# Second expert choice over 54 key-score sums, and places turned into rows and columns by steps, in a two-layer encoder with product-key experts

## The chip, the core and the metric

The kernel runs on one core of a Trainium2 chip, in one launch. The metric is the device time of one execution in microseconds (us), lower is better. TensorE does the matrix products, VectorE (DVE) and ScalarE (ACT) the elementwise work, GpSimd (POOL) issues the indirect DMAs here, and SyncE (SP) the plain DMAs. Each engine works through its own queue in order.

## The reference, cut to what matters

256 tokens of width 1024 pass through two layers. Each has a token mixer (two attention branches, left out here) and a product-key expert layer, which the change touches:

```python
q = (xc @ w_query).reshape(T, 8, 2, 128)              # 8 heads, two half queries
s = einsum('thpk,pnk->thpn', q, sub_keys)             # 128 key scores for each half
sv, si = lax.top_k(s, 16)
cand = sv[:, :, 0, :, None] + sv[:, :, 1, None, :]    # 16 x 16 sums
cidx = si[:, :, 0, :, None] * 128 + si[:, :, 1, None, :]
top_s, sel = lax.top_k(cand, 16)                      # the second choice, of 256
eidx = take_along_axis(cidx, sel)
g = softmax(top_s)
act = gelu(einsum('td,thkd->thk', x, expert_down[eidx]))
out = einsum('thk,thkd->td', g * act, expert_up[eidx])
```

Since both lists of 16 are sorted, the sum at place (a, b) can be among the 16 largest only if (a+1)(b+1) is at most 16.

## The kernel before

**Products.** All weights stream in units of 128 x 1024 values (512 KB). Each is split into a rounded part `wh` (ScalarE, L194) and a rest `wl` (VectorE, L197), up to four units ahead, and TensorE multiplies three combinations of parts. In the expert layer the down weights of all 16384 experts are multiplied (128 units, two to a block, 64 blocks, L1326, products at L1338 to L1340, 24 to a unit). Of the up weights, the rows that some token uses are gathered in an order found on the chip and multiplied at L1372.

**Choosing experts**, while query and down products run: `score_lane` (L929) makes the key scores. `topk_lane` (L943) has eight steps per layer (four head pairs by two chunks of 128 tokens). In each, `top16` (L909: two rounds of the eight largest, their places, and a replacement of the first eight) sorts four rows of 128 scores in two pairs, then two rows of 256 sums (made at L958). `index_lane` (L966) follows when the eighth step is done, chunk by chunk: it parts each chosen place (0 to 255) into row and column by a shift and a mask, compares these with 0 to 15 (`i16`, L989), multiplies by the key numbers (L992), and adds up 16 values by halving sums (L995: 1024, 512, 256 and 128 values). TensorE then turns the result round (L1005) and it goes to `ijT` and `gT` (the last at L1015). When both chunks are through, `done["idx"]` is set; before block 32 the down products require it (`main_need("idx")`, L1329).

**From `idx` on.** `gate_lane` (L1091) starts the gate groups (`gate_group`, L1026): one-hot matrices on VectorE and ScalarE and products of them on TensorE, 44 groups for list 0 (80 of the 128 rows of experts), then 32 for list 1. `rank_lane` (L1107) counts which experts are used and ranks them when the last group of a list is done (products at L1134, L1139 and L1143, between them a ScalarE copy at L1136). `send_lane` (L1166) then has GpSimd send the 80 (or 40) rows of gate times activation to their ranked places (L1183). `read_back` (L1201) reads a list's rows back when all its sends have landed, `split_rows` (L1247) splits them (L1259, L1261), the number read with a row gathers its up weights (L1243), and `Stream._prep` (L186) splits those at L194 and L197.

**Order.** A planner in the kernel's Python (`Lanes`, L67) writes out one order for all engines. It has a clock each for TensorE ("p"), VectorE ("v") and ScalarE ("s"). A lane is a generator whose `yield ("v", cost)` says what the instructions behind it cost. A step is put in when its engine's clock and the lane's due time are at most `far` ahead of "p" (4.0 us, 6.0 for the splits), and its lane is due again 0.15 after it. `main` adds the products' cost to "p" (0.7 for a quarter of a down unit) and lets the lanes go on. `vcost(n)` is 0.1 + 0.00105 n; a split costs 1.14 of "v". The costs set the order alone, the chip its own times.

Of the kernel before, what the change touches and what calls it, by code (L numbers as in the profile page):

```python
# [12 lines left out]
F16 = mybir.dt.float16  # L13
U32 = mybir.dt.uint32
AF = mybir.ActivationFunctionType
OP = mybir.AluOpType
# [14 lines left out]
NU_W = 34 + 8 + 8 + 16  # L31


C_ID, C_IOTA, C_I16, C_COS, C_SIN, C_MA, C_MB, C_END = 0, 128, 256, 272, 400, 528, 592, 1104


GSCALE, LOW = 2.0 ** 15, 2.0 ** -11
NQ = 4
AHEAD = 4

# [18 lines left out]
def vcost(n):  # L59
    return 0.1 + n * 0.00105  # L60
# [159 lines left out]
def encoder_kernel(ctx, tc, x_in, wts, downs, ups, gains, gate_bias, qk_norm, rpb, sink, skeys, consts, sums, out,  # L220
                   depth=DEPTH):
    nc = tc.nc
    ctx.enter_context(tc.manual_schedule())
    cpool = ctx.enter_context(tc.tile_pool(name="cpool", bufs=1))
# [74 lines left out]
    x = cpool.tile([128, 2, D], F32, name="x")  # L299
    cst = cpool.tile([128, C_COS], F32, name="cst")  # L300
    TT = cpool.tile([128, 2, 2, 8, 128], F32R, name="TT")
    TTf = TT.rearrange("p c l k t -> p (c l k t)")
    iota2 = cpool.tile([128, 128, 2], F16, name="iota2")
    i16 = cpool.tile([128, 8, 2], F16, name="i16")
    tiny = cpool.tile([128, 2], F32, name="tiny")
    rank = cpool.tile([128, 128], U32, name="rank")
    miss = cpool.tile([128, 4], F16, name="miss")
# [160 lines left out]
    for l in range(depth):  # L468
# [5 lines left out]
        if l == 0:  # L474
            g1n = z[:, 0, 0:4, :].rearrange("p a b -> p (a b)")
            nc.sync.dma_start(g1n, bcast_row(gains, 0, D))
            nc.sync.dma_start(cst, consts[:, 0:C_COS])
            st.load(0)
            nc.sync.dma_start(x[:, 1, :], x_in[128:256, :])
            st.load(3)  # L480

            nc.vector.memset(iota2, 0.0)
            z2 = iota2.rearrange("p a b -> p (a b)")
            warm = take("s")
            for n in range(40):
# [12 lines left out]
            nc.vector.tensor_copy(iota2, cst[:, C_IOTA:C_IOTA + 128][:, :, None].to_broadcast([128, 128, 2]))  # L498
            nc.vector.tensor_copy(i16.rearrange("p a s -> p (a s)"), cst[:, C_I16:C_I16 + 16])
            acc_first = first_half(u, "T1")  # L500

        ctab = ap.tile([128, C_END - C_COS], F32, name="ctab")
# [373 lines left out]
        def area(off, n, u32=False):  # L876
            return (afu if u32 else afl)[:, A0 + off:A0 + off + n]
# [45 lines left out]
        sv = [area(M + ch * 768, 256).rearrange("p (q k) -> p q k", k=16) for ch in range(2)]  # L923
# [3 lines left out]
        M2 = M + 1536  # L927
# [15 lines left out]
        def topk_lane():  # L943
            for n in range(8):
                cg, ch = n // 2, n % 2
                yield from lane_need([("s", cg, ch)])
                sc = area(4096 + n * 512, 512).rearrange("p (q n) -> p q n", n=128)
                s2 = area(8192 + (n % 2) * 512, 512).rearrange("p (q n) -> p q n", n=128)
                cd = area(9216 + (n % 2) * 512, 512).rearrange("p (h a b) -> p h a b", h=2, b=16)
                c2 = area(10240 + (n % 2) * 512, 512).rearrange("p (h ab) -> p h ab", h=2)  # L950
                for k in range(0, 4, 2):
                    yield ("v", 2.0)
                    top16([(sv[ch][:, 4 * cg + j, :], si[ch][:, 4 * cg + j, :], sc[:, j, :], s2[:, j, :])
                           for j in (k, k + 1)])
                yield ("v", 0.7)
                for hh in range(2):
                    h = 2 * cg + hh
                    nc.vector.tensor_tensor(cd[:, hh], sv[ch][:, 2 * h, :, None].to_broadcast([128, 16, 16]),  # L958
                                            sv[ch][:, 2 * h + 1, None, :].to_broadcast([128, 16, 16]), op=OP.add)
                yield ("v", 3.4)  # L960
                top16([(ts[ch][:, 2 * cg + hh, :], sel[ch][:, 2 * cg + hh, :],
                        cd[:, hh].rearrange("p a b -> p (a b)"), c2[:, hh]) for hh in range(2)])
                if n == 7:
                    done["top"] = 0.0

        def index_lane():  # L966
            yield from lane_need(["top"])
            for ch in range(2):
                w = lambda k: area(M2 + k * 128, 128).rearrange("p (h k) -> p h k", k=16)
                wu = lambda k: area(M2 + k * 128, 128, True).rearrange("p (h k) -> p h k", k=16)  # L970
                sif = area(M2 + 8 * 128, 128).bitcast(F16).rearrange("p (h q k) -> p h q k", q=2, k=16)
                wh = lambda k: area(M2 + k * 128, 128).bitcast(F16).rearrange("p (n s) -> p n s", s=2)
                yield ("v", 0.6)
                nc.vector.tensor_tensor(w(0), ts[ch], ts[ch][:, :, 0:1].to_broadcast([128, 8, 16]), op=OP.subtract)
                nc.vector.tensor_copy(sif, si[ch].rearrange("p (h q) k -> p h q k", q=2))
                te = yield ("s", 0.3)
                nc.scalar.activation(w(0), w(0), AF.Exp)
                yield ("v", 0.8)
                nc.vector.tensor_scalar(wu(1), sel[ch], 4, None, op0=OP.logical_shift_right)
                nc.vector.tensor_scalar(wu(7), sel[ch], 15, None, op0=OP.bitwise_and)  # L980
                for k in range(2):
                    nc.vector.tensor_copy(wh(2 + k), area(M2 + (1, 7)[k] * 128, 128, True)[:, :, None].to_broadcast(
                        [128, 128, 2]))
                for q in range(2):

                    eq = area(11264, 1024).bitcast(F16).rearrange("p (n a s) -> p n a s", a=8, s=2)
                    e4 = area(11264, 1024).bitcast(F16).rearrange("p (h k a) -> p h k a", h=8, a=16)
                    yield ("v", vcost(1024) + 0.3)
                    nc.vector.tensor_tensor(eq, wh(2 + q)[:, :, None, :].to_broadcast([128, 128, 8, 2]),  # L989
                                            i16[:, None, :, :].to_broadcast([128, 128, 8, 2]), op=OP.is_equal)  # L990
                    yield ("v", vcost(1024))
                    nc.vector.tensor_mul(e4, e4, sif[:, :, q, None, :].to_broadcast([128, 8, 16, 16]))  # L992
                    for m in (8, 4, 2, 1):
                        yield ("v", vcost((64 if m > 1 else 128) * m))
                        nc.vector.tensor_add(w(4 + q)[:, :, :, None] if m == 1 else e4[:, :, :, 0:m], e4[:, :, :, 0:m],  # L995
                                             e4[:, :, :, m:2 * m])
                sm = area(M2 + 7 * 128, 8)
                yield ("v", 0.8)
                nc.vector.tensor_reduce(sm, w(0), axis=AX.X, op=OP.add)
                nc.vector.reciprocal(sm, sm)  # L1000
                nc.vector.tensor_mul(w(6), w(0), sm[:, :, None].to_broadcast([128, 8, 16]))
                b, = yield from lane_take("t")
                yield ("p", 0.65)
                for k in range(3):
                    nc.tensor.transpose(b[:, k * 128:(k + 1) * 128], area(M2 + (4 + k) * 128, 128), ident)  # L1005
                cs = slice(ch * 128, (ch + 1) * 128)
                yield ("s", 0.6)
                nc.scalar.activation(ijT[:, :, cs], b[:, 0:256].rearrange("p (a t) -> p a t", a=2), AF.Copy)
# [317 lines left out]
        for b in range(64):  # L1326
# [4 lines left out]
            for ii in range(2):  # L1331
                h, lo = st.get(u)
# [167 lines left out]
def const_table():  # L1500
    c = np.zeros((128, C_END), np.float32)
    c[:, C_ID:C_ID + 128] = np.eye(128, dtype=np.float32)
    c[:, C_IOTA:C_IOTA + 128] = np.arange(128, dtype=np.float32)[None]
    c[:, C_I16:C_I16 + 16] = np.arange(16, dtype=np.float32)[None]
    half = DH // 2
    inv = np.float32(10000.0) ** (-np.arange(half, dtype=np.float32) / np.float32(half))
    ang = np.arange(T, dtype=np.float32)[:, None] * inv[None, :].astype(np.float32)
# [36 lines left out]
```

## Time and profile before

| what | before |
|---|---|
| median of 3 runs | 1828.98 us (1825.52 to 1829.77) |
| the profiled execution | 1823.0 us, its span 1821.2 us |
| TensorE busy | 1774.6 us (97%) |
| VectorE busy | 1476.7 us (81%) |
| ScalarE busy | 1084.8 us (60%) |
| GpSimd busy | 503.6 us (28%) |
| DMA | 377.4 MB, 207 GB/s in the mean |

The span is the profiled execution from its first to its last instruction, and the time has 1.8 us more around it. Issuing instructions and waits are not counted as busy. Matmuls overlap in their pipeline and their ends are modelled.

### The profile page before, as it was taken

To read this page: it belongs to the slowest core of one execution; us is meant where nothing else is said; L and a number is where in the kernel's file an instruction comes from. 1 tells how busy PE (TensorE), PEld (TensorE's weight loads), DVE (VectorE), ACT (ScalarE), POOL (GpSimd) and SP (SyncE) were. 2 spreads that over 40 slices of the span, in tenths; PEclk is the share of its full clock that TensorE was granted. 3 is DMA by queue.
4 is the path that set the end of the run, shared out by engine and by line. 5 is a ranking of instruction groups with operands and counts; after the bars stand their busy time and mean duration, and the time that the engine had idled before them with its cause. 6 is when DMAs were issued, how large, how long until landed. Compare 5 with 4: busy or idle time off the path is not lost. (4 is left out here: it accounts for less than half of the span.)

```text
span 1821.2 us, 37929 instructions
## 1 busy us (share of the span) xinstructions
PE 1774.6 (97%) x14646; PEld 1619.0 (89%) x14646; DVE 1476.7 (81%) x3196; ACT 1084.8 (60%) x1784; POOL 503.6 (28%) x448
## 2 busy tenths in 40 slices
PE   8999999999999989999999999999999999799998
PEld 7889899999999978878778988999999999788786
DVE  6986799998888967766689768999888889677665
ACT  5675554676557646665646654546665577466554
POOL 0000000000007777775200000000000177677661
PEclk9999999999999989999999999999999999899999
DMA  7535455544547869989564354556444588699893
GB/s 258 162 114 167 149 155 184 196 157 149 160 143 239 250 216 349 322 303 342 190 213 143 106 164 162 162 182 201 149 153 153 158 240 250 244 327 321 302 324 129
DMA packets 130518, 377.40 MB, mean 207 GB/s; under 512 B 17552, under 2 KB 43792, under 8 KB 130320
## 3 DMA queue, kind: packets, MB, share of 16 engines
q1 hardware_dynamic: 90288, 239.26, 42.7%
q0 software_dynamic: 40032, 135.54, 20.5%
q8 instruction: 119, 1.95, 0.4%
q14 instruction: 79, 0.65, 0.1%
HBM read 341.98 MB, written 32.75 MB: 206 GB/s over the span
## 5 line engine op out<-in xcount | busy, mean ns | idle before, releaser
L197 DVE TENSOR_TENSOR wl<-raw,wh 128x1024 fp32r<-128x1024 f32 x476 | 577.9, 1222 | 144.1 <-ACT wh L194 135.7
L194 ACT ACTIVATE wh<-raw 128x1024 fp32r<-128x1024 f32 x476 | 503.1, 1058 | 252.7 <-PE bank L1372 60.9
L1338 PE MATMUL bank<-TT,wh 128*128 128x256 f32 x2048 | 586.2, 286 | 0.0
L1340 PE MATMUL bank<-TT,wl 128*128 128x256 f32 x2048 | 572.9, 280 | 2.2 <-DVE wl L197 2.2
L1339 PE MATMUL bank<-TT,wh 128*128 128x256 f32 x2048 | 571.8, 279 | 0.0
L1340 PEld LDWEIGHTS bank<-TT,wl 128*128 128x128 f32 x2048 | 385.6, 188 | 3.9 <-DVE wl L197 3.9
L1339 PEld LDWEIGHTS bank<-TT,wh 128*128 128x128 f32 x2048 | 385.8, 188 | 0.0
L1338 PEld LDWEIGHTS bank<-TT,wh 128*128 128x128 f32 x2048 | 385.2, 188 | 0.3
L1372 PE MATMUL bank<-wh,TT 128*128 128x512 f32 x1296 | 358.4, 396 | 5.1 <-DVE TT L1261 2.1
L1183 POOL DMA_INDIRECT rows<-act,rank x240 | 280.6, 1169 | 92.5 <-issue 62.8
L1372 PEld LDWEIGHTS bank<-wh,TT 128*128 128x128 f32 x1296 | 242.3, 188 | 69.5 <-DVE TT L1261 6.1
L881 POOL IOTA act<- 128x128 uint32 (+2 forms) x6 | 2.0, 332 | 1080.0 <-PE bank L361 410.2
L197 DVE TENSOR_TENSOR wl<-act,wh 128x1024 fp32r<-128x1024 f32 x126 | 154.4, 1226 | 81.3 <-ACT wh L194 81.2
L1372 PE MATMUL bank<-wl,TT 128*128 128x512 f32 x648 | 204.8, 395 | 0.8 <-issue 0.8
L194 ACT ACTIVATE wh<-act 128x1024 fp32r<-128x1024 f32 x126 | 133.4, 1060 | 103.0 <-PE bank L1372 90.0
L1243 POOL DMA_INDIRECT act<-in_ups_dram,act x118 | 132.3, 1121 | 74.2 <-issue 28.1
L1372 PEld LDWEIGHTS bank<-wl,TT 128*128 128x128 f32 x648 | 121.7, 188 | 29.4
L441 PE MATMUL bank<-TT,wh 128*128 128x256 f32 x448 | 128.6, 287 | 2.0 <-ACT raw_ka L570 1.0
L443 PE MATMUL bank<-TT,wh 128*128 128x256 f32 x448 | 125.1, 279 | 0.0
L444 PE MATMUL bank<-TT,wl 128*128 128x256 f32 x448 | 125.0, 279 | 0.0
L1282 ACT ACTIVATE act<-bank 128x256 f32<-128x256 f32 (+12 forms) x214 | 65.5, 351 | 80.3 <-PE bank L1340 78.0
L1043 ACT ACTIVATE oh<-oh 128x1024 f16<-128x1024 f16 (+2 forms) x108 | 102.0, 958 | 14.5 <-DVE oh L1040 13.4
(262 smaller groups left out, 2835.7 us busy)
## 6 DMA issues: line engine op xcount, KB each, us to landing
raw<-in_downs_dram SPq DMA_DIRECT2D x256, 512.0 KB, 3.7
raw<-in_wts_dram SPq DMA_DIRECT2D x132, 512.0 KB, 4.3
act<-rows SPq DMA_DIRECT2D x100, 129.0 KB, 5.0
act<-rows SPq DMA_DIRECT2D x98, 64.5 KB, 5.1
act<-in_ups_dram SPq DMA_DIRECT2D x8, 512.0 KB, 7.3
raw<-in_ups_dram SPq DMA_DIRECT2D x8, 512.0 KB, 6.5
rows<-act,rank POOLq DMA_INDIRECT x240, 5.0
act<-in_ups_dram,act POOLq DMA_INDIRECT x118, 6.8
```

The costliest lines, as they stand in the source:

```text
L194: self.nc.scalar.activation(h, r, AF.Copy)
L197: self.splits.append(self.nc.vector.tensor_sub(lo, r, h.bitcast(F32)).ins.name)
L441: nc.tensor.matmul(o, wh, rh, start=first and i == 0 and pc == 0, stop=False, skip_group_check=True)
L443: nc.tensor.matmul(o, wh, rl, start=False, stop=False, skip_group_check=True)
L444: nc.tensor.matmul(o, wl, rh, start=False, stop=last and i == len(kcs) - 1 and pc == 1, skip_group_check=True)
L1043: nc.scalar.activation(el, ej, AF.Copy, scale=LOW)
L1183: snd = nc.gpsimd.indirect_dma_start(byrank[r], bass.IndirectOffsetOnAxis(ap=rank[:, i:i + 1], axis=0), afl[:, i * ROW:(i + 1) * ROW], None)
L1243: nc.gpsimd.indirect_dma_start(w, None, ups_rows, bass.IndirectOffsetOnAxis(ap=num, axis=0), element_offset=l * 16384 * D)
L1338: nc.tensor.matmul(o, lh, TT[:, :, 0, kc, :], start=kc == 0, stop=False)
L1339: nc.tensor.matmul(o, lh, TT[:, :, 1, kc, :], start=False, stop=False)
L1340: nc.tensor.matmul(o, ll, TT[:, :, 0, kc, :], start=False, stop=kc == 7)
L1372: nc.tensor.matmul(oacc[ch][hf], a, r[:, hf * 512:(hf + 1) * 512], start=first[hf] and a is lh and r is h, stop=last and a is ll)
```

## The change

The second choice is taken from 54 sums instead of 256. `STEPS` lists rectangles (first row, rows, columns): one row with 16 columns, one with 8, two with 5, four with 3 and eight with 1. These hold every place with (a+1)(b+1) up to 16. Five additions, each for two heads, write them one behind the other, and `top16` sorts rows of 54.

A place is now a number from 0 to 53, and row and column no longer come from a shift and a mask. For each place all 16 row starts (`c16[:, 1]`) are compared with it (`is_ge`). The outcome times the differences of successive row keys (`dif`), added up, gives the row's key number; times the differences of successive row starts (`c16[:, 2]`), added up, it gives the start of its row. The place less that start is the column, which is compared with 0 to 15 as before. There are three times four halving sums per chunk instead of twice four, and five passes over 2048 f16 values instead of four. A second buffer of 1024 words holds the outcome of the comparison. The costs in the `yield`s change with it. The constant table has 32 more columns.

```diff
+STEPS = [(0, 1, 16), (1, 1, 8), (2, 2, 5), (4, 4, 3), (8, 8, 1)]
+CANDS = sum(n * m for _, n, m in STEPS)
...
-                cd = area(9216 + (n % 2) * 512, 512).rearrange("p (h a b) -> p h a b", h=2, b=16)
-                c2 = area(10240 + (n % 2) * 512, 512).rearrange("p (h ab) -> p h ab", h=2)
+                cd = area(9216 + (n % 2) * 512, 2 * CANDS).rearrange("p (h c) -> p h c", h=2)
+                c2 = area(10240 + (n % 2) * 512, 2 * CANDS).rearrange("p (h c) -> p h c", h=2)
...
-                yield ("v", 0.7)
-                for hh in range(2):
-                    h = 2 * cg + hh
-                    nc.vector.tensor_tensor(cd[:, hh], sv[ch][:, 2 * h, :, None].to_broadcast([128, 16, 16]),
-                                            sv[ch][:, 2 * h + 1, None, :].to_broadcast([128, 16, 16]), op=OP.add)
-                yield ("v", 3.4)
...
+                yield ("v", 0.9)
+                s4 = sv[ch][:, 4 * cg:4 * cg + 4, :].rearrange("p (h q) k -> p h q k", q=2)
+                c0 = 0
+                for a0, na, nb in STEPS:
+                    shape = [128, 2, na, nb]
+                    nc.vector.tensor_tensor(cd[:, :, c0:c0 + na * nb].rearrange("p h (a b) -> p h a b", a=na),
+                                            s4[:, :, 0, a0:a0 + na, None].to_broadcast(shape),
+                                            s4[:, :, 1, None, 0:nb].to_broadcast(shape), op=OP.add)
+                    c0 += na * nb
+                yield ("v", 2.2)
+                top16([(ts[ch][:, 2 * cg + hh, :], sel[ch][:, 2 * cg + hh, :], cd[:, hh], c2[:, hh])
+                       for hh in range(2)])
...
-                yield ("v", 0.6)
+                yield ("v", 1.2)
                 nc.vector.tensor_tensor(w(0), ts[ch], ts[ch][:, :, 0:1].to_broadcast([128, 8, 16]), op=OP.subtract)
                 nc.vector.tensor_copy(sif, si[ch].rearrange("p (h q) k -> p h q k", q=2))
+
+                nc.vector.tensor_copy(dif[:, :, 0:1], sif[:, :, 0, 0:1])
+                nc.vector.tensor_sub(dif[:, :, 1:16], sif[:, :, 0, 1:16], sif[:, :, 0, 0:15])
                 te = yield ("s", 0.3)
                 nc.scalar.activation(w(0), w(0), AF.Exp)
-                yield ("v", 0.8)
-                nc.vector.tensor_scalar(wu(1), sel[ch], 4, None, op0=OP.logical_shift_right)
-                nc.vector.tensor_scalar(wu(7), sel[ch], 15, None, op0=OP.bitwise_and)
...
+                yield ("v", 0.3)
+                nc.vector.tensor_copy(pl(1), sel[ch].rearrange("p h k -> p (h k)")[:, :, None].to_broadcast([128, 128, 2]))
...
+                yield ("v", vcost(1024))
+                nc.vector.tensor_tensor(g8, pl(1)[:, :, None, :].to_broadcast([128, 128, 8, 2]),
+                                        c16[:, 1, None, :, :].to_broadcast([128, 128, 8, 2]), op=OP.is_ge)
+                yield ("v", vcost(1024))
+                nc.vector.tensor_mul(e4, g4, dif[:, :, None, :].to_broadcast([128, 8, 16, 16]))
+                yield from total(w(4)[:, :, :, None])
+
+                yield ("v", vcost(1024))
+                nc.vector.tensor_mul(e8, g8, c16[:, 2, None, :, :].to_broadcast([128, 128, 8, 2]))
+                yield from total(pl(2).rearrange("p (h k) s -> p h k s", h=8)[:, :, :, 0:1])
+                yield ("v", 0.6)
+                nc.vector.tensor_sub(pl(3)[:, :, 0:1], pl(1)[:, :, 0:1], pl(2)[:, :, 0:1])
+                nc.vector.tensor_copy(pl(3)[:, :, 1:2], pl(3)[:, :, 0:1])
+                yield ("v", vcost(1024))
+                nc.vector.tensor_tensor(e8, pl(3)[:, :, None, :].to_broadcast([128, 128, 8, 2]),
+                                        c16[:, 0, None, :, :].to_broadcast([128, 128, 8, 2]), op=OP.is_equal)
+                yield ("v", vcost(1024))
+                nc.vector.tensor_mul(e4, e4, sif[:, :, 1, None, :].to_broadcast([128, 8, 16, 16]))
+                yield from total(w(5)[:, :, :, None])
```

`total` is the four halving sums, each behind its own `yield ("v", vcost(...))`, with the last one into the place given.

## Rows read from the trace of the kernel before

**Rows 1.** The page, busy us, share of the span and instructions of each engine.
```profile
PE 1774.6 (97%) x14646; PEld 1619.0 (89%) x14646; DVE 1476.7 (81%) x3196; ACT 1084.8 (60%) x1784; POOL 503.6 (28%) x448
```
**Rows 2.** Waits of weight loads, whole span: total us, times, longest.
```profile
PEld L1143 <- ACT scr L1136: 19.1, 2, 10.0
...
PEld bank L1340 <- DVE wl L197: 3.9, 8, 0.6
```
**Rows 3.** The same view, from 205 to 350 us.
```profile
PEld bank L1340 <- DVE wl L197: 2.0, 4, 0.6
```
**Rows 4.** Stretches: busy us (instructions) of PE, PEld, DVE, ACT, POOL, clock, DMA.
```profile
211.00:321.00 110.00, 109.21 (x926) 108.60 (x925) 109.91 (x435) 53.38 (x75) 0.00 (x0) 1.00 0.52 164
321.00:366.50 45.50, 45.13 (x384) 44.92 (x384) 43.43 (x69) 28.19 (x43) 0.37 (x1) 1.00 0.61 195
...
660.00:680.00 20.00, 11.03 (x99) 10.13 (x98) 7.68 (x23) 5.76 (x11) 11.88 (x13) 0.74 0.74 243
```
**Rows 5.** Timeline, ScalarE, 658 to 690 us: start, us, instruction, idle before.
```profile
666.95 0.61 ACT L1259 ACTIVATE wh<-act 128x256 fp32r<-128x256 f32 x2 [5.34 <-DMA act<-rows]
673.14 1.06 ACT L194 ACTIVATE wh<-raw 128x1024 fp32r<-128x1024 f32 x1 [5.58 <-DMA raw<-in_ups_dram,act]
674.10 0.57 ACT L1136 ACTIVATE scr<-bank 40x512 f16<-40x512 f32 x1
```
**Rows 6.** GpSimd: first and last send of layer 0, and their group.
```profile
544.20 2.15 POOL L1183 DMA_INDIRECT rows<-act,rank  x1 [9.70 <-DVE miss L1155]
...
662.17 0.96 POOL L1183 DMA_INDIRECT rows<-act,rank  x1 [0.30 <-issue]
...
L1183 POOL DMA_INDIRECT rows<-act,rank x80 | 94.9, 1186 | 33.8 <-issue 18.6 <-DVE miss L1155 9.7 <-DVE oh L1049 4.0
```
**Rows 7.** Timeline, TensorE, 674 to 679 us.
```profile
674.73 0.51 PE L1143 MATMUL bank<-scr 40*128 40x40 f16 x10 [8.97 <-ACT scr L1136]
...
677.69 0.41 PE L1340 MATMUL bank<-TT,wl 128*128 128x256 f32 x1
...
677.99 0.89 PE L1372 MATMUL bank<-wh 128*128 128x512 f32 x2
```
**Rows 8.** Timeline, VectorE, index lane of layer 0.
```profile
320.93 2.33 DVE L197 TENSOR_TENSOR wl<-raw,wh 128x1024 fp32r<-128x1024 f32 x2
...
352.19 2.18 DVE L995 TENSOR_TENSOR act<-act 128x1024 f16<-128x1024 f16 x4
...
365.78 0.23 DVE L1015 TENSOR_SCALAR gT<-act 128x128 f16<-128x128 f32 x1
```
**Rows 9.** Timeline, VectorE, one step of the top-k lane.
```profile
237.21 0.48 DVE L912 MAX8 act<-act 128x8 f32<-128x128 f32 x2
...
239.56 1.21 DVE L197 TENSOR_TENSOR wl<-raw,wh 128x1024 fp32r<-128x1024 f32 x1
...
244.16 0.75 DVE L958 TENSOR_TENSOR act<-act 128x256 f32<-128x256 f32 x2
244.82 0.74 DVE L912 MAX8 act<-act 128x8 f32<-128x256 f32 x2
...
248.51 2.34 DVE L197 TENSOR_TENSOR wl<-raw,wh 128x1024 fp32r<-128x1024 f32 x2
250.76 0.48 DVE L912 MAX8 act<-act 128x8 f32<-128x128 f32 x2
```
**Rows 10.** Timeline, VectorE, two small steps of the rank lane.
```profile
535.65 0.20 DVE L1128 TENSOR_TENSOR scr<-scr 128x80 f16<-128x80 f16 x1
535.77 0.19 DVE L1129 TENSOR_TENSOR scr<-scr 128x80 f16<-128x80 f16 x1
```
**Rows 11.** Groups by form: count, busy us, mean ns, idle before.
```profile
L197 DVE TENSOR_TENSOR wl<-raw,wh 128x1024 fp32r<-128x1024 f32 x476 | 577.9, 1222 | 144.1 <-ACT wh L194 135.7 <-DVEq L1387 5.0
...
L958 DVE TENSOR_TENSOR act<-act 128x256 f32<-128x256 f32 x32 | 12.1, 422 | 0.0
...
L989 DVE TENSOR_TENSOR act<-act,i 128x2048 f16<-128x2048 f16 x8 | 9.8, 1220 | 0.1
```

More of the change, by code (lines that the diff above doesn't have):

```diff
@@ L31 @@
 NU_W = 34 + 8 + 8 + 16
-C_ID, C_IOTA, C_I16, C_COS, C_SIN, C_MA, C_MB, C_END = 0, 128, 256, 272, 400, 528, 592, 1104
+C_ID, C_IOTA, C_I16, C_COS, C_SIN, C_MA, C_MB, C_END = 0, 128, 256, 304, 432, 560, 624, 1136
 GSCALE, LOW = 2.0 ** 15, 2.0 ** -11
+STEPS = [(0, 1, 16), (1, 1, 8), (2, 2, 5), (4, 4, 3), (8, 8, 1)]
+CANDS = sum(n * m for _, n, m in STEPS)
 NQ = 4
@@ L303, in encoder_kernel @@
     iota2 = cpool.tile([128, 128, 2], F16, name="iota2")
-    i16 = cpool.tile([128, 8, 2], F16, name="i16")
+    c16 = cpool.tile([128, 3, 8, 2], F16, name="c16")
     tiny = cpool.tile([128, 2], F32, name="tiny")
@@ L498, in encoder_kernel @@
             nc.vector.tensor_copy(iota2, cst[:, C_IOTA:C_IOTA + 128][:, :, None].to_broadcast([128, 128, 2]))
-            nc.vector.tensor_copy(i16.rearrange("p a s -> p (a s)"), cst[:, C_I16:C_I16 + 16])
+            nc.vector.tensor_copy(c16.rearrange("p n a s -> p (n a s)"), cst[:, C_I16:C_I16 + 48])
             acc_first = first_half(u, "T1")
@@ L954, in topk_lane @@
                            for j in (k, k + 1)])
-                yield ("v", 0.7)
-                for hh in range(2):
-                    h = 2 * cg + hh
-                    nc.vector.tensor_tensor(cd[:, hh], sv[ch][:, 2 * h, :, None].to_broadcast([128, 16, 16]),
-                                            sv[ch][:, 2 * h + 1, None, :].to_broadcast([128, 16, 16]), op=OP.add)
-                yield ("v", 3.4)
-                top16([(ts[ch][:, 2 * cg + hh, :], sel[ch][:, 2 * cg + hh, :],
-                        cd[:, hh].rearrange("p a b -> p (a b)"), c2[:, hh]) for hh in range(2)])
+                yield ("v", 0.9)
[10 more added lines that the diff above has]
+                       for hh in range(2)])
                 if n == 7:
@@ L971, in index_lane @@
                 sif = area(M2 + 8 * 128, 128).bitcast(F16).rearrange("p (h q k) -> p h q k", q=2, k=16)
-                wh = lambda k: area(M2 + k * 128, 128).bitcast(F16).rearrange("p (n s) -> p n s", s=2)
-                yield ("v", 0.6)
+                dif = area(M2 + 9 * 128, 64).bitcast(F16).rearrange("p (h k) -> p h k", h=8)
+                pl = lambda k: area(M2 + k * 128, 128).bitcast(F16).rearrange("p (n s) -> p n s", s=2)
+                yield ("v", 1.2)
                 nc.vector.tensor_tensor(w(0), ts[ch], ts[ch][:, :, 0:1].to_broadcast([128, 8, 16]), op=OP.subtract)
@@ L981, in index_lane @@
[L981 to L992, printed above, removed]
+                yield ("v", 0.3)
@@ L993, in index_lane, with total @@
+                nc.vector.tensor_copy(pl(1), sel[ch].rearrange("p h k -> p (h k)")[:, :, None].to_broadcast([128, 128, 2]))
+                ge, eq = [area(11264 + k * 1024, 1024).bitcast(F16) for k in range(2)]
+                g8, e8 = [x.rearrange("p (n a s) -> p n a s", a=8, s=2) for x in (ge, eq)]
+                g4, e4 = [x.rearrange("p (h k a) -> p h k a", h=8, a=16) for x in (ge, eq)]
+                def total(dst):
                     for m in (8, 4, 2, 1):
                         yield ("v", vcost((64 if m > 1 else 128) * m))
-                        nc.vector.tensor_add(w(4 + q)[:, :, :, None] if m == 1 else e4[:, :, :, 0:m], e4[:, :, :, 0:m],
-                                             e4[:, :, :, m:2 * m])
+                        nc.vector.tensor_add(dst if m == 1 else e4[:, :, :, 0:m], e4[:, :, :, 0:m], e4[:, :, :, m:2 * m])
@@ L1503, in const_table @@
     c[:, C_IOTA:C_IOTA + 128] = np.arange(128, dtype=np.float32)[None]
-    c[:, C_I16:C_I16 + 16] = np.arange(16, dtype=np.float32)[None]
+    first = np.concatenate([[0], np.cumsum(sum(([m] * n for _, n, m in STEPS), []))[:-1]])
+    c[:, C_I16:C_I16 + 48] = np.concatenate([np.arange(16), first, np.diff(first, prepend=0)])[None]
     half = DH // 2
```

## Prediction

> **What bounds the kernel now.** The page first: TensorE is busy in 97% of the span, VectorE in 81% [rows 1]. So VectorE time as such is worth nothing; what counts is where TensorE stands still, 46.6 us in all (1821.2 less 1774.6). I therefore read the waits of TensorE and its weight loads next. One of them is large: in each layer the products at L1143 wait some 9.5 us for ScalarE's copy at L1136, 19.1 us in two waits [rows 2]. A smaller one bears on the changed code: a down product (L1340) waits for VectorE's `wl` (L197) eight times, 3.9 us [rows 2], and four of these, 2.0 us, lie in layer 0 between 205 and 350 us [rows 3]; the other four stand in the same stretch of layer 1.
>
> The stretches say why. While the key scores are sorted (211 to 321 us) VectorE is busy 109.9 of 110 us, so the splits that TensorE needs come late; in the index stretch behind it 43.4 of 45.5 us [rows 4].
>
> The large wait is 300 us later and has another cause. In the slice from 660 to 680 us TensorE is busy 11.0 of 20 us and its granted clock falls to 0.74 of full speed [rows 4]. ScalarE's queue has, in this order, the splits of the first rows read back (L1259, idle 5.3 us for a DMA), the split of the first gathered up block (L194, idle 5.6 us for the gather) and then L1136 [rows 5]. The gather waits for rows read back, and those for the last of 80 row sends. The sends run on GpSimd one behind the other from 544.2 to 663.1 us: 94.9 us of work and about 0.3 us between two, which is 119 us for 80 [rows 6]. They start when the first list's ranks are known, at the end of the gate groups, which start at `done["idx"]`. So **the time at which the index lane ends, in TensorE's own program, sets when the stall at L1143 ends** (674.7 us) [rows 7], as long as gates and sends keep their lengths. Nothing waits at `main_need("idx")`: the index lane ends at 366 us [rows 8], and block 32 is some 179 us of products behind the first (32 times two units of 2.8 us), which begins only after the 12 query units that run beside the first sorts.
>
> **The change, part by part. Sorting on the engine.** One step of the top-k lane (eight a layer) runs from 237.2 to 250.8 us [rows 9]. A pair of 128-wide sorts takes 2.35 us (237.21 to 239.56), the two 256-wide sums 0.66, the 256-wide sorts 3.69 (244.82 to 248.51). Ten sort instructions lose (3.69-2.35)/128 = 10.5 ns per column together, so 54 columns cost 3.69 - 202 x 0.0105 = 1.6 us if the line holds; at worst they cost as much as the 128-wide ones, 2.35. The five small sums (16 to 32 values each) show nowhere; the nearest rows are 80-wide f16 steps of 0.2 us started 0.12 us apart [rows 10], against 0.33 us for a 256-wide sum, so 5 x 0.13 = 0.65, at most 5 x 0.42 = 2.1 [rows 11]. I take the line and 0.65, since the operands are small and independent: a step falls by 3.69 + 0.66 - 1.6 - 0.65 = 2.1 us (bounds -0.1 and 2.2), 16 steps by 33.6 us.
>
> [...]
>
> **Index lane on the engine.** Added per chunk: one cast and two shifts less (some 0.4 together, at the 0.12 to 0.2 of small steps [rows 10]), one full pass more (1.22 [rows 11]; five for four), one chain of four halving sums more (2.1 us [rows 8]; three for two), four small copies and subtractions, 0.2 each. That is +1.2 + 2.1 + 0.8 - 0.4 = +3.7 us, four times: +14.8. Net VectorE -19 us of 1476.7. That alone would give back only the late splits.
>
> **In the planner.** The order on TensorE comes from the costs in the `yield`s. Units cost it 4 x 0.7 = 2.8 us of "p" and 1.14 us of "v", and a lane of this priority may run only 4 us ahead of "p". A lane that has only "v" work therefore moves at (2.8-1.14)/2.8 = 0.59 of TensorE's time. The trace bears it out: a sorting step costs 2+2+0.7+3.4 = 8.1, which gives 13.7 us, and it takes 13.55 [rows 9]. After: 2+2+0.9+2.2 = 7.1. Eight steps: 8 x 1.0/0.593 = 13.5 us earlier per layer.
> The index costs 0.6 + 0.8 + 2 x (1.475 + 1.175 + 1.475) + 0.8 + 0.6 = 11.05 per chunk (1.175 a pass, 1.475 the four sums), which gives 37 us for two; the trace has 45 from 321 to 366 [rows 8], the rest being 0.15 us between two steps of a lane and two trips through TensorE and ScalarE that stay. After: 1.2 + 0.3 + 5 x 1.175 + 3 x 1.475 + 0.6 + 0.8 + 0.6 = 13.8. With six steps more per chunk, of which I count four with their 0.15 (where no split steps between), it is 2.75 + 0.6 = 3.35 a chunk, 2 x 3.35/0.593 = 11.3 us later. **Net: `idx` 2.2 us earlier per layer.** Bounds: no gap counted, 13.5 - 9.3 = +4.2; all six, +1.2; and one unit (2.8 us) to either side, since steps land between units: -1.6 to +7.
>
> **Sum.** The late splits go: before, a step wants 9.05 us of sorting (13.55 less four splits, 4.5 us [rows 9]) and 4.9 units' splits, 14.6 us in the 13.7 us it is given, 0.9 short, and eight such make the 2 us that TensorE waits. After, 6.95 + 4.28 x 1.13 = 11.8 in 12.0: no arrears. In the index stretch 43.4 + 7.4 + 4 more splits (4.6) = 55.4 us in 45.5 + 11.3 = 56.8: close, but what is left is covered by splits made up to four units ahead. So ranks, sends and gathers come 2.2 + 2.0 us earlier, and the stall at L1143 ends that much earlier. The 2.0 us of waits are not counted a second time: TensorE comes to the stall 2.0 us sooner, and the stall itself is 2.2 us shorter (9.0 to 6.8). Two layers: 3.9 + 4.4 = 8.3 us. The profiled execution, 1823.0 us, becomes 1814.7; it lies 6 us under the median of 1829.0, from which I take the same 8.3: **1820.7 us**. The wider constant table (32 columns more of a load of 272) and the masks' new offset cost nothing: the first transposes wait for x and its norm too, and 16 KB more is 0.1 us at the mean 207 GB/s of the page.
>
> **Rivals.** *A, more:* if the second list's ranks come about 3 us earlier in the planner's order, L1136 is put ahead of L194 on ScalarE. Then TensorE does L1143 and its last 12 down products in the wait, which now run after it, from 675.2 to 677.9 us at the lower clock [rows 7, 4], and starts the up blocks as soon as the first is split (674.2 [rows 5] and 1.2 for its `wl` [rows 11], 675.4). That is 1 to 3 us more per layer; with the 4.2 and up to 1.2 for a clock that does not fall, 10 to 17 us in all: 1812 to 1819. For it: the distance is one unit. Against: my 2.2 us fall short of it.
> *B, nothing:* the planner's steps in the index lane eat all of the sorting's gain (net 0 or one unit late); then only the late splits go, 3.9 us less up to 3.9 us given back: 1825 to 1829.
> *C, slower:* the new f16 passes (`is_ge` and products against `c16` and `dif`) run at one value a cycle. The f32 rows give 1.04 us per 1000 values ((1222-422)/768 ns [rows 11]), so a pass of 2048 takes 2.29 us instead of 1.22, ten of them 10.7 us a layer. VectorE then ends the index 9.3 us late (10.7 less the 1.4 spare), and the gate groups' products, which have no cover of units ahead, wait for it: 9.3 - 4.2 = 5 us a layer, 1839 us. It decides from about 2.1 us a pass. Against it stands L989, whose broadcast operands have the same form and which takes 1.22.
> [...]
>
> **Chances.** Forecast (gain of 5.5 to 11 us) 0.45, A beyond it 0.18, B 0.26, C and other orders that come out later 0.11. A measurement of this kernel tells about 0.3%, 5.5 us, from no change. Faster 0.63, same 0.26, slower 0.11. The range goes from A's far side to B's end and a noise of 1 us: 1812 to 1830; the forecast's own is 1818 to 1823.5.
>
> **What would show it.** Right: the sort instructions at 54 columns near 0.21 us; the waits of L1340 on L197 in the sorting stretch gone; VectorE under 110 of 110 us there; the first send of layer 0 near 540 instead of 544.2 us with 119 us to the last; the wait at L1143 near 7 us; VectorE at about 1458 us. Wrong: sends that start at the same time or later (the planner's count failed), sends that take longer (GpSimd waits on something else), passes above 1.22 us, or a stall that moves from L1143 to L1372 with its length kept.

## The result and the profile after

The changed kernel took 1816.92 us (median of 7 runs, 1815.12 to 1823.4), the kernel before 1825.58 us (7 runs beside them): a ratio of 0.9949 [0.9934, 0.9964], which is 9.3 us (8.7 between the medians). The profiled execution is the one of 1816.92 us, with a span of 1815.1 us against 1821.2, 6.1 us less. The forecast was a gain of 8.3 us. The size came out; the way to it did so only in part. The forecast's time, 1820.7 us, was taken from a median of three runs of the kernel before, 1828.98; with seven it is 3.4 us lower, and so the time measured lies inside the whole range (1812 to 1830) but under the forecast's own (1818 to 1823.5), while the gain lies in the one forecast (5.5 to 11).

The page, busy time of each engine:

```profile
PE 1777.3 (98%) x14646; PEld 1637.2 (90%) x14646; DVE 1452.2 (80%) x3270; ACT 1085.9 (60%) x1792; POOL 495.4 (27%) x448
```

VectorE has lost 24.5 us [rows 1]. TensorE has the same 14,646 products, is busy 2.7 us longer and stands still 37.8 us instead of 46.6.

Stretches of layer 0, columns as in [rows 4]:

```profile
211.00:321.00 110.00, 110.00 (x923) 110.00 (x922) 102.85 (x475) 55.96 (x77) 0.00 (x0) 1.00 0.54 169
321.00:366.50 45.50, 45.50 (x382) 45.50 (x382) 41.84 (x69) 26.73 (x43) 0.37 (x1) 1.00 0.60 186
660.00:680.00 20.00, 14.55 (x164) 13.57 (x164) 10.96 (x28) 8.19 (x16) 10.67 (x11) 0.87 0.71 230
```

TensorE now stands nowhere while the scores are sorted, and VectorE has 7 us of slack there. Yet TensorE's products in the first stretch are 923, not more than the 926 of before, although it is busy 0.8 us longer [rows 4]. That is the first sign of something that the prediction did not hold.

Timeline of VectorE, one step of the top-k lane, and then groups by form, columns as in [rows 11]:

```profile
238.05 0.54 DVE L964 TENSOR_TENSOR act<-act 128x32 f32<-128x32 f32 x5
238.63 0.33 DVE L916 MAX8 act<-act 128x8 f32<-128x54 f32 x2
...
240.25 1.21 DVE L201 TENSOR_TENSOR wl<-raw,wh 128x1024 fp32r<-128x1024 f32 x1
```
```profile
L918 DVE FIND_INDEX8 act<-act 128x8 uint32<-128x54 f32 x32 | 6.3, 208 | 0.0
...
L964 DVE TENSOR_TENSOR act<-act 128x16 f32<-128x16 f32 x32 | 5.4, 169 | 0.0
...
L1004 DVE TENSOR_TENSOR act<-act,c 128x2048 f16<-128x2048 f16 x4 | 4.9, 1225 | 0.1
L1007 DVE TENSOR_TENSOR act<-act 128x2048 f16<-128x2048 f16 x4 | 4.9, 1225 | 0.1
```

The five sums take 0.58 us and the sorts over 54 sums 1.62 (238.63 to 240.25), beside 0.66 and 3.69 before. The new full passes take 1.22 us each.

Waits of the weight loads over the whole span; the line for a down product behind `wl` (before 3.9 us in eight, [rows 2]) is gone, and the large wait has another name:

```profile
PEld L1159 <- DVE scr L1153: 10.3, 2, 5.7
```

Timelines around that wait: GpSimd (first send, last send, first gather), ScalarE and TensorE.

```profile
543.80 2.15 POOL L1208 DMA_INDIRECT rows<-act,rank  x1 [9.81 <-DVE miss L1180]
...
661.15 1.19 POOL L1208 DMA_INDIRECT rows<-act,rank  x1 [0.30 <-issue]
...
668.64 0.97 POOL L1268 DMA_INDIRECT raw<-in_ups_dram,act  x1 [6.30 <-DVE wh L1286]
```
```profile
665.52 0.20 ACT L1105 ACTIVATE act<-bank 128x32 f32<-128x32 f32 x1 [3.37 <-PE bank L1092]
...
667.68 0.62 ACT L1284 ACTIVATE wh<-act 128x256 fp32r<-128x256 f32 x2 [0.33 <-DMA act<-rows]
674.05 1.06 ACT L198 ACTIVATE wh<-raw 128x1024 fp32r<-128x1024 f32 x1 [5.75 <-DMA raw<-in_ups_dram,act]
```
```profile
671.72 0.28 PE L1365 MATMUL bank<-TT,wl 128*128 128x256 f32 x1
677.45 0.68 PE L1159 MATMUL bank<-scr 128*40 128x128 f16 x4 [5.45 <-DVE scr L1153]
678.06 1.22 PE L1397 MATMUL bank<-wh 128*128 128x512 f32 x2
```

The sends start 0.4 us earlier than before, not 4.2 [rows 6], and the first up product starts 0.07 us later (677.99 before, [rows 7]). So up to 678 us layer 0 has gained nothing. Its last up product starts at 912.96 us instead of 916.45. The gain of layer 0, 3.5 us, appears in 235 us of up products that the change does not touch. Windows of one stretch of down and one of up products, first the kernel before, then the changed one:

```profile
380.00:520.00 140.00, 140.00 (x1584) 138.53 (x1584) 124.98 (x246) 88.92 (x159) 0.00 (x0) 1.00 0.49 153
740.00:760.00 20.00, 20.00 (x87) 16.14 (x86) 14.01 (x19) 13.09 (x20) 15.69 (x15) 1.00 0.97 321
```
```profile
380.00:520.00 140.00, 140.00 (x1566) 138.50 (x1566) 123.12 (x243) 87.68 (x157) 0.00 (x0) 1.00 0.48 151
740.00:760.00 20.00, 20.00 (x90) 16.57 (x89) 14.22 (x21) 13.14 (x20) 15.73 (x15) 1.00 0.98 339
```

TensorE is busy all of the time at a granted clock of 1.00 in all four, and yet does 18 products fewer in 140 us of down blocks and 3 more in 20 us of up blocks. The mean gap from the start of one product to the next, worked out from the timeline, went from 117.1 to 119.7 ns for the down products (L1363 to L1365, before L1338 to L1340) and from 233.3 to 226.9 for the up products (L1397, before L1372). This gap is called the pace below. It counts gaps up to 160 and up to 300 ns, since longer ones hold a wait or another product.

### The profile page after: what moved, and what is told of

The parts are those of the page before. It is cut to its first block, busy times and chain, and to the rows that moved or that the text cites. A ratio compares the mean times of both kernels' runs of the same rounds, so it can differ in the third digit from the quotient of the medians.

```text
span 1815.1 us, 38007 instructions
## 1 busy us (share of the span) xinstructions
PE 1777.3 (98%) x14646; PEld 1637.2 (90%) x14646; DVE 1452.2 (80%) x3270; ACT 1085.9 (60%) x1792; POOL 495.4 (27%) x448
## 5 line engine op out<-in xcount | busy, mean ns | idle before, releaser
L1363 PE MATMUL bank<-TT,wh 128*128 128x256 f32 x2048 | 591.7, 289 | 0.0
L1364 PE MATMUL bank<-TT,wh 128*128 128x256 f32 x2048 | 578.9, 283 | 0.0
L1365 PE MATMUL bank<-TT,wl 128*128 128x256 f32 x2048 | 578.4, 282 | 0.0
L1364 PEld LDWEIGHTS bank<-TT,wh 128*128 128x128 f32 x2048 | 392.0, 191 | 0.0
L1365 PEld LDWEIGHTS bank<-TT,wl 128*128 128x128 f32 x2048 | 391.8, 191 | 0.0
L1363 PEld LDWEIGHTS bank<-TT,wh 128*128 128x128 f32 x2048 | 391.4, 191 | 0.0
L1397 PE MATMUL bank<-wh,TT 128*128 128x512 f32 x1296 | 350.2, 390 | 6.2 <-DVE TT L1286 2.2
L1397 PEld LDWEIGHTS bank<-wh,TT 128*128 128x128 f32 x1296 | 242.2, 188 | 62.2 <-DVE TT L1286 5.4
L1397 PE MATMUL bank<-wl,TT 128*128 128x512 f32 x648 | 200.6, 389 | 1.5 <-issue 1.5
L1268 POOL DMA_INDIRECT act<-in_ups_dram,act x118 | 126.6, 1073 | 71.3 <-issue 30.2
L1397 PEld LDWEIGHTS bank<-wl,TT 128*128 128x128 f32 x648 | 121.6, 188 | 25.4
L445 PE MATMUL bank<-TT,wh 128*128 128x256 f32 x448 | 130.1, 290 | 1.6 <-ACT raw_ka L574 1.0
L447 PE MATMUL bank<-TT,wh 128*128 128x256 f32 x448 | 126.6, 283 | 0.0
L448 PE MATMUL bank<-TT,wl 128*128 128x256 f32 x448 | 126.6, 283 | 0.0
L1307 ACT ACTIVATE act<-bank 128x256 f32<-128x256 f32 (+9 forms) x216 | 66.1, 350 | 84.7 <-PE bank L1365 82.2
L1109 DVE TENSOR_TENSOR act<-act,bank 128x480 f32<-128x480 f32 (+32 forms) x152 | 71.3, 471 | 51.8 <-ACT act L1105 45.8
```

The source lines that it names most:

```text
L445: nc.tensor.matmul(o, wh, rh, start=first and i == 0 and pc == 0, stop=False, skip_group_check=True)
L447: nc.tensor.matmul(o, wh, rl, start=False, stop=False, skip_group_check=True)
L448: nc.tensor.matmul(o, wl, rh, start=False, stop=last and i == len(kcs) - 1 and pc == 1, skip_group_check=True)
L1109: nc.vector.tensor_mul(a, a, bv[:, 0:g])
L1268: nc.gpsimd.indirect_dma_start(w, None, ups_rows, bass.IndirectOffsetOnAxis(ap=num, axis=0), element_offset=l * 16384 * D)
L1363: nc.tensor.matmul(o, lh, TT[:, :, 0, kc, :], start=kc == 0, stop=False)
```

## The experiments

Theory: where the tiles lie sets that pace. `cst` is 128 bytes a partition longer in the changed kernel and `c16` 64 longer than `i16`; so TT, which both kinds of product read, begins at byte 10560 instead of 10432, and the first `wh` at 47936 instead of 47744: 37376 apart instead of 37312. The rival: the pace follows from what VectorE and ScalarE do, which the new algorithm changes. The runs stood on three chips. On two of them (the first four runs and the last four) TensorE idles 60 to 73 us in all under `issue`, that is, while it waits for nothing that the profile shows, and the kernel before takes 1932.4 and 1948.9 us; ratios there are to runs of the kernel before on the same chip, and order and pace are read from the traces.

**Place alone and algorithm alone.** `e1_place` has the algorithm of before at the new places:

```diff
-C_COS, C_SIN, C_MA, C_MB, C_END = 272, 400, 528, 592, 1104
+C_COS, C_SIN, C_MA, C_MB, C_END = 304, 432, 560, 624, 1136
-    i16 = cpool.tile([128, 8, 2], F16, name="i16")
+    c16 = cpool.tile([128, 3, 8, 2], F16, name="c16")
+    i16 = c16[:, 0]
```

> The kernel before, with nothing of the change but its places in memory: the constant table 32 columns wider and the small f16 constant three times as large, so that the transposed activations TT lie 128 bytes and the weight buffers wh and wl 192 bytes further on. Order theory (the gain comes from the earlier ranks alone): as before, ratio 1.000, down products 118 ns apart and up products 226 ns apart, as in the profile of before. Place theory (where the operands lie sets the pace of the matmuls): the paces of the changed kernel, 120 ns for the down products and 220 ns for the up products; slower downs make the ranks some 4 us later per layer, faster ups (972 of them a layer) give back some 6 us per layer, so the time is 1 to 2 us less per layer, ratio 0.998, and the first send of layer 0 lies near 548 us instead of 544.

`e2_oldplace` has the changed algorithm at the old places: `c16` lies in columns of the table that are free by then and is filled by four small steps.

```diff
-C_COS, C_SIN, C_MA, C_MB, C_END = 304, 432, 560, 624, 1136
+C_COS, C_SIN, C_MA, C_MB, C_END = 272, 400, 528, 592, 1104
-    c16 = cpool.tile([128, 3, 8, 2], F16, name="c16")
+    i16 = cpool.tile([128, 8, 2], F16, name="i16")
+    c16 = cst[:, C_IOTA + 72:C_IOTA + 96].bitcast(F16).rearrange("p (n a s) -> p n a s", n=3, s=2)
```

> The changed kernel, with every tile at the address it has in the kernel before (the new constants lie inside the part of the constant table that is free after the first copy; four small copies more at the start). Order theory: as the changed kernel, ratio 0.995 to before, paces 120 and 220 ns. Place theory: paces 118 and 226 ns as before; the ranks then come the full 4 us earlier (first send of layer 0 near 540 us), the up products lose 6 us a layer against the changed kernel, so ratio 0.995 to 0.997, the same gain by another way: all of it at the stall, none in the up products.

The paces followed the places: 120.0 (from 211 to 321 us) and 227.3 ns in `e1_place`, with the algorithm of before, and 117.8 and 233.4 in `e2_oldplace`, with the new one. The rival falls. The expectations put the two paces of the up products at 226 and 220 ns; they are 233 and 227, with the same difference. The ranks of the first list (its first product) came at 541.1 us in `e1_place` and 535.1 in `e2_oldplace`, against 539.4 in the kernel before's own profile. The whole times were 1.0036 [1.0012, 1.0061] and 1.0017 [0.9990, 1.0043]: this chip shows no gain of the algorithm, and both ratios lie above what was expected (0.998, and 0.995 to 0.997). Its idle time under `issue` stands in TensorE's waits (`e1_place`; the kernel before has 0.8 us of it in its profile):

```profile
PE bank L1373 <- issue: 15.8, 18, 2.3
PE bank L1068 <- issue: 13.2, 23, 1.2
```

**What the planner is told.** `e3_oldcosts` is the changed kernel with the old costs in two `yield`s, `e4_steps256` has all 256 sums as well and keeps the new index lane:

```diff
-                yield ("v", 0.9)
+                yield ("v", 0.7)
...
-                yield ("v", 2.2)
+                yield ("v", 3.4)
```
```diff
-STEPS = [(0, 1, 16), (1, 1, 8), (2, 2, 5), (4, 4, 3), (8, 8, 1)]
+STEPS = [(0, 16, 16)]
```

> The changed kernel with the planner's old costs for the sorting step (0.7 and 3.4 in place of 0.9 and 2.2); the instructions are the same, only their order differs. Order theory: the index lane ends 13.5 us later per layer than in the changed kernel, ranks and sends likewise (first send of layer 0 near 557 us), and the up products start about that much later: 1830 to 1842 us, ratio 1.003 to 1.010. Rival (VectorE's saved work is the gain): as the changed kernel, ratio 0.995.

> The index lane by steps alone: all 256 sums are kept (one rectangle of 16 by 16, in one addition for two heads), with the planner's old costs for the sorting step; five passes and three chains of sums per chunk as in the changed kernel. Order theory: the index lane ends 11 us later per layer than before and the sends with it (first send of layer 0 near 555 us), the late splits of the sorting stretch are back, 4 us of waits at L1340's counterpart: ratio 1.008 to 1.013. Rival (TensorE is the bound and VectorE's work beside it is hidden): ratio 1.000.

Measured: 1.0103 [1.0056, 1.0150] and 1.0108 [1.0052, 1.0163], with the ranks at 550.2 and 549.7 us, 11 us after the changed kernel's. The first send of `e3_oldcosts`:

```profile
555.09 2.14 POOL L1208 DMA_INDIRECT rows<-act,rank  x1 [8.06 <-DVE miss L1180]
```

VectorE from 211 to 321 us, `e3_oldcosts` and then `e4_steps256` (columns as in [rows 4]):

```profile
211.00:321.00 110.00, 110.00 (x923) 110.00 (x922) 97.44 (x463) 53.08 (x74) 0.00 (x0) 1.00 0.53 172
211.00:321.00 110.00, 109.91 (x918) 109.56 (x918) 109.76 (x417) 53.85 (x77) 0.00 (x0) 1.00 0.50 162
```

Two numbers in the `yield`s, with no instruction changed, move the ranks by 11 us. VectorE is idle for 12.6 us of the stretch in the one and for 0.2 in the other, and the ranks come within 0.5 us of each other. So the order that the planner writes sets them, not VectorE's work: in both runs 94.0 units of 24 down products stand ahead of the ranks in TensorE's row, 4.25 more than in the changed kernel, and 44.75 ahead of the index lane's end, 5.25 more (13.5 us, or 4.8 units, by the prediction's reckoning). The late splits that `e4_steps256` was to bring back cost 0.9 us in four waits, not 4.

**The same on a chip without this idle time.** `e7_changed` is the changed kernel, `e8_oldplace` is `e2_oldplace`.

> The changed kernel itself, to stand beside the two below on one chip. Both theories: ratio 0.995 to before, paces 120 (down) and 220 ns (up).

> The changed kernel at the addresses of the kernel before, once more, beside the changed kernel. Place theory with the planner's shift: paces 118 and 226 ns, the first list's ranks 4 us earlier than in before and in the changed kernel, the up products 2.7% slower than in the changed kernel (6 us a layer); ratio to before 0.994 to 0.997. Order theory alone: the same as the changed kernel in every row.

The kernel before took 1824.63 us (13 runs). `e7_changed`: 1817.19, 0.9958 [0.9941, 0.9975]. `e8_oldplace`: 1818.76, 0.9963 [0.9952, 0.9973]. Here the algorithm alone gains 5.9 us between the medians (6.8 by the ratio), and the new places add nothing that the intervals tell apart. Within the kernel the two differ as the places want it. `e8_oldplace`: the two windows of above, GpSimd (first and last send, first gather), ScalarE and TensorE:

```profile
380.00:520.00 140.00, 140.00 (x1583) 138.49 (x1582) 124.70 (x245) 87.40 (x155) 0.00 (x0) 1.00 0.47 154
740.00:760.00 20.00, 20.00 (x88) 16.10 (x87) 13.82 (x19) 12.12 (x20) 15.73 (x15) 1.00 0.97 327
```
```profile
540.60 2.15 POOL L1214 DMA_INDIRECT rows<-act,rank  x1 [10.12 <-DVE miss L1186]
...
658.05 0.96 POOL L1214 DMA_INDIRECT rows<-act,rank  x1 [0.31 <-issue]
...
663.73 0.97 POOL L1274 DMA_INDIRECT raw<-in_ups_dram,act  x1 [4.72 <-DVE wh L1292]
```
```profile
662.77 0.67 ACT L1290 ACTIVATE wh<-act 128x256 fp32r<-128x256 f32 x2 [1.46 <-DMA act<-rows]
```
```profile
672.88 0.68 PE L1165 MATMUL bank<-scr 128*40 128x128 f16 x4 [7.06 <-DVE scr L1159]
673.49 1.22 PE L1403 MATMUL bank<-wh 128*128 128x512 f32 x2
```

With the places held, the sends start 3.6 us earlier and the up products 4.5 us earlier than in the kernel before [rows 6, 7]: the prediction's chain. But the last up product starts only 2.2 us earlier (914.27 against 916.45). Most of the difference of 2.3 us arises in the first 20 us of up products, before and then `e8_oldplace`:

```profile
678.00:698.00 20.00, 20.00 (x87) 16.24 (x87) 16.20 (x24) 13.34 (x21) 14.92 (x15) 0.99 1.04 395
```
```profile
673.50:693.50 20.00, 20.00 (x90) 15.63 (x90) 15.85 (x28) 12.86 (x20) 15.10 (x14) 0.92 1.04 397
```

The columns count all products; of up products there are 85 and 77, and 8 at 233 ns are 1.9 us. Before, TensorE came out of the stall with 12 down products left, which ran ahead of the first up product, 0.21 us apart at a granted clock of 0.50 (675.2 to 677.7 us). Now they are done ahead of the stall, and the up products take that place: in `e8_oldplace` the ones from 674.51 to 676.22 us start 0.43 us apart instead of 0.233. The clock of 0.92 in place of 0.99, 0.07 of 20 us, is 1.4 us. The rest goes with 12 products of the second list's ranks, which before ran ahead of the up products and now stand among them. From the 20th up product to the 500th the two kernels keep step (2.0 us apart); over all 990 it is 2.3. In the changed kernel itself the clock of these 20 us is 0.91 (0.50 from 678 to 681 us), with 78 up products.

**What of the place matters.** `e5_pad64` moves TT and everything behind it by 64 bytes more, which leaves their distance as it is; `e6_pad64_64` moves what lies behind TT by another 64, so that the distance is 37440.

```diff
-C_COS, C_SIN, C_MA, C_MB, C_END = 304, 432, 560, 624, 1136
+C_COS, C_SIN, C_MA, C_MB, C_END = 320, 448, 576, 640, 1152
```
```diff
+    pad = cpool.tile([128, 16], F32, name="pad")
     tiny = cpool.tile([128, 2], F32, name="tiny")
```

> The changed kernel with 16 more unused columns in the constant table, so that TT and the weight buffers both lie 64 bytes further on than in the changed kernel (both then start at a multiple of 128; before, TT starts 64 past one and the buffers at one; in the changed kernel both 64 past one). If the pace hangs on how TT lies against the weight buffers: 120 and 220 ns, ratio 0.995. If it hangs on each start by itself: other paces, the downs between 113 and 120, the ups between 213 and 226, and a ratio that follows them. If place is nothing: 0.995.

> As the run with 16 more columns, and another 64 unused bytes between TT and the weight buffers: TT starts at a multiple of 128 and the buffers 64 past one, the two the other way round than before. If the pace hangs on how they lie against each other: 118 and 226 ns, ratio 0.995 to 0.997. If on each by itself: other paces. If place is nothing: 0.995.

`e5_pad64`: 1816.77 us, 0.9956 [0.9940, 0.9973], with the paces of the changed kernel. `e6_pad64_64`: 1800.27 us (1792.5 to 1807.0), 0.9857 [0.9818, 0.9896], faster than both kernels, with 117.7 ns for the down products from 211 to 321 us and 115.8 over all, and 229.0 for the up products. No outcome named in its expectation has such a gain. Its page, the same two windows as above, and its first send:

```profile
PE 1755.9 (97%) x14646; PEld 1610.2 (89%) x14646; DVE 1451.3 (81%) x3270; ACT 1085.7 (60%) x1792; POOL 502.0 (28%) x448
```
```profile
380.00:520.00 140.00, 140.00 (x1609) 138.59 (x1605) 125.08 (x244) 89.13 (x157) 0.00 (x0) 1.00 0.48 155
740.00:760.00 20.00, 20.00 (x89) 16.43 (x88) 14.09 (x20) 12.53 (x21) 15.73 (x15) 1.00 0.96 322
```
```profile
535.95 2.15 POOL L1209 DMA_INDIRECT rows<-act,rank  x1 [10.27 <-DVE miss L1181]
```

TensorE does the same 14,646 products in 21.4 us less than in the changed kernel. By the paces, 6144 down products at 3.9 ns less are 24 us and 1980 up products at 2.1 ns more take 4 back. The padding is worth more than the change.

**Again on a chip with idle time under `issue`**, for the gain without the change and for the period of the effect. `e9_place` is `e1_place`; its expectation supposes a chip where TensorE does not wait for its instructions; the run had 60.6 us of the idle time, and no run shows what that waits for. `e10_before_pad128` is the kernel before and `e11_pad128` the changed kernel with `pad` of 32 columns (128 bytes: distances 37440 and 37504); `e12_pad192` is the changed kernel with one of 48 (37568).

> The kernel before at the changed kernel's addresses, once more, on a chip where TensorE does not wait for its instructions. If the change's gain is its planner's shift and the saved late splits: downs at 120 ns and ups at 219 ns, first list's ranks 2 to 4 us later than before, up products 4 us a layer shorter, in sum ratio 0.998 to 1.001. If the gain is the place alone: 0.995.

> The kernel before with 128 unused bytes between TT and the weight buffers and nothing else, so that they lie 37440 bytes apart, as in the run that was 1.4% faster than before. If the pace hangs on that distance: downs 116 and ups 220 ns, 6144 x 1.5 ns less for the downs (as far as the stall does not eat them) and 1950 x 4 ns less for the ups: ratio 0.990 to 0.995, without anything of the change. If the gain of that run belongs to the changed kernel's order: 1.000.

> The changed kernel with TT and the weight buffers 37504 bytes apart (128 more than in the changed kernel). If the pace hangs on the distance with a period of 128 bytes: as the changed kernel, 119.7 and 218 ns, 0.996. If the period is longer: other paces, between 113 and 120 and between 213 and 226 ns, and a ratio between 0.98 and 1.00 that follows them.

> The changed kernel with TT and the weight buffers 37568 bytes apart (192 more than in the changed kernel; 256 more than before). With a period of 128 bytes: as the run at 37440, 116 and 220 ns, 0.986. With a period of 256: as at the distance of the kernel before, 117 and 224 ns, 0.996.

Measured: `e9_place` 1.0017 [0.9987, 1.0047], `e10_before_pad128` 0.9945 [0.9921, 0.9969], `e11_pad128` 1.0038 [1.0007, 1.0070], `e12_pad192` 0.9996 [0.9972, 1.0020]. Only `e10_before_pad128` has the ratio expected of it if the pace hangs on the distance: the kernel before with the pad alone is faster than without. `e9_place` was to be at most 1.001, `e11_pad128` 1.00, and `e12_pad192` 0.996 for a period of 256. The paces of all kernels but `e3_oldcosts` and `e4_steps256`, which have the changed kernel's distance (from 211 to 321 us they do 923 and 918 products, it does 923); early is from 211 to 321 us:

| distance `wh` to TT, bytes (rest by 256) | kernels | down products, ns (early / all) | up products, ns |
|---|---|---|---|
| 37312 (192) | before, e2, e8 | 117.8 / 117.1 to 117.6 | 233.3 to 233.4 |
| 37376 (0) | changed, e1, e5, e7, e9 | 120.0 / 119.7 to 119.8 | 226.9 to 227.3 |
| 37440 (64) | e6; e10 | 117.7 / 115.8; 115.2 / 115.5 | 229.0; 229.3 |
| 37504 (128) | e11 | 120.0 / 119.1 | 232.6 |
| 37568 (192) | e12 | 117.8 / 117.2 | 233.3 |

The distance orders the paces over all, whatever the algorithm and the chip. It does not tell everything: `e6_pad64_64` and `e10_before_pad128` have the same distance, with both buffers 192 bytes further on in the first, and differ by 2.5 ns early. A period of 128 bytes falls: 37376 and 37504 differ in the up products, 37312 and 37440 in both. Of a period of 256, one pair (37312 and 37568) shows the return.

## Why the prediction was right, and where not

- **Sorting.** A step's sums and sorts fell by 2.15 us (forecast 2.1). The line through the 128- and 256-wide sorts gave 1.6 us for 54 columns, measured 1.62. The late splits are gone.
- **Small steps.** Alone each of the five sums has a row of 169 to 182 ns, 0.87 us in all, but the five together take 0.58 us, because they overlap; my 0.65 was near. VectorE fell to 1452.2 us, forecast about 1458: the lines of the sorting lost 35.5 us (forecast 33.6), those of the index lane added 13.7 (forecast 14.8), and the rest of the difference lies in lines that the change does not touch and in overlaps. The step on slices of `dif` that start at an odd value (120 f16 values, L987) took 224 ns, beside 288 for an f32 step of 128 values (L983).
- **The planner's order.** Counted in units of 24 down products that stand ahead in TensorE's row, the index lane's end came 1.25 units (3.5 us) earlier, at 39.5 instead of 40.75, and the first list's ranks 1 unit earlier, at 89.75 instead of 90.75. The forecast was 2.2 us, 0.8 units. With the 2.0 us of late splits that makes 4.2 us; `e8_oldplace` shows 3.7 at the ranks and 4.5 at the first up product. This step is shown, as is the reason: the costs in the `yield`s move the ranks by 11 us by themselves. In the changed kernel the sends start at 543.8 us, near 544.2 and not 540, which the prediction had named as the sign that the planner's count failed. The count held; the slower down products hid it.
- **"The wider constant table and the masks' new offset cost nothing."** This step failed. I priced the load of the table and not where the tiles behind it come to lie. The new places made the down products 2.2 to 2.5 ns slower in the mean, which took back 3.2 us up to the ranks (538.9 against 535.7 us in `e8_oldplace`) and 4.6 up to the first up product, and the up products some 6.4 ns faster, which gave 5.9 us back over the up blocks (234.9 against 240.8). In sum the places gave nothing that can be told: `e8_oldplace` and the changed kernel stand within each other's intervals. So the algorithm's gain has about the forecast's size, but in the changed kernel it appears at other places than the forecast's. That the two effects of the places nearly cancel was luck: `e6_pad64_64` is 1.0% faster than `e5_pad64`, and `e11_pad128` 0.4% slower than `e12_pad192`, by their places.
- **"As long as gates and sends keep their lengths."** The sends did (117 to 118 us from first to last start). The second list's gates did not: in the planner's order their last group came 0.75 units later, and the list's first product behind all 128 units instead of one unit ahead of the end. The large wait therefore moved from L1143 to that first product (L1159), and VectorE's and ScalarE's parts of the last two groups now stand ahead of the split of the rows read back. In the changed kernel the first gather went out at 668.64 us, 7.5 us behind the last send's start; in the kernel before that was 5.7 and in `e8_oldplace` 5.7 too. `e8_oldplace` has the changed kernel's order, so the order alone does not cost this: there ScalarE still waited 1.5 us for the rows, while in the changed kernel it came to them late, behind a group's products that the slower pace had put off, and waited 0.33. The forecast of about 7 us for the wait came out at 5.45, and at 7.06 with the old places.
- **Rival A** put the down products into the wait; they did go there (they end at 671.72 us), but because the list came later and not earlier, and the first up product came no sooner. What A wanted to save at the low clock (0.50 from 675.2 to 677.7 us before) was moved to the up products: their first 20 us ran at a granted clock of 0.91. **Rival B** falls in the planner's order, **rival C** by the passes of 1.22 us: at the f32 rows' 1.04 us per 1000 values they would have taken 2.29 (that this is one value a cycle, no run shows).
- **Open.** Why the distance sets the pace: it was shown only which distances go with which pace, and padding moved `raw`, `wh`, `wl` and all the rest behind TT together, so that the pair that matters was not singled out. And on the two chips where TensorE idles under `issue` the algorithm's gain was not seen (`e2_oldplace` 1.0017, `e12_pad192` 0.9996 at paces like those of before); the traces there show the ranks as early as elsewhere, but where the gain went behind them was not followed, nor what the idle time waits for. On the chip without it the algorithm of before was not run at the new places.

## What to carry to other kernels

An edit that changes the size of one long-lived tile can move the tiles behind it, as here TT by 128 bytes and the first `wh` by 192, with the down products' pace from 117.1 to 119.7 ns: compare the pace of untouched products before and after, and test the edit once at the old places, before a gain or a loss is put down to the algorithm. Where TensorE bounds the kernel, try pads of 64 bytes and more between the operands by themselves; here one gave more than the change (`e6_pad64_64` 1800.27 us, `e5_pad64` 1816.77), and with another (`e11_pad128`) the changed kernel was 0.4% slower than the kernel before. And when a planner's order holds a long chain, count the units ahead of each mark in TensorE's row for every list, since one lane that moves up can push another back.

## What the runs showed of the hardware

With TensorE busy without a gap at a granted clock of 1.00, 256-column products started 115 to 120 ns apart and 512-column ones 227 to 233, by where the buffers lay and nothing else that was changed. Distances were tried in steps of 64 bytes; the best for the one kind (37440) was not the best for the other (37376). The granted clock was below 1.00 around the stall: 0.74 in its stretch before [rows 4], 0.50 from 675.2 to 677.7 us there, where down products started 0.21 us apart, and 0.91 and 0.92 in the first 20 us of up products of the changed kernel and `e8_oldplace`. The kernel before took 6 to 7% longer on two of the three chips of the experiments (1932.4 and 1948.9 us against 1824.6), where the profiles show 60 to 73 us of TensorE's idle time under `issue`, against 0.5 to 1.3 on the third.
